# The down projection by a seven-product scheme on one NeuronCore

## The chip, the cores and the metric

The kernel runs on one core of one Trainium2 chip. The metric is device time in microseconds (us) of the whole program, the median of several runs. The engines are named as the profile names them: PE is TensorE (matmuls; PEld its weight loads), DVE VectorE, ACT ScalarE, POOL GpSimd, SP SyncE, which here issues the DMAs.

## The reference

One layer of a hybrid encoder on 1024 tokens of width 1024: gated attention and a state-space branch, cross-attention, then a squared-ReLU MLP with a hidden width of 4096, and a final norm. The change concerns the last matrix product alone:

```
h = rmsnorm(x, norm_ffn[i])
x = x + jnp.square(jax.nn.relu(h @ w_up[i])) @ w_down[i]
...
return rmsnorm(x, norm_final)
```

All is float32. The kernel multiplies float32 by three matmuls: an operand is split into a high half (a copy into the fp32r type) and a low half (the operand minus its high half), and high x high, high x low and low x high are added up in PSUM.

## The kernel before, in words

The up phase leaves u = relu(h w_up)^2, transposed, in DRAM as 32 rows of tiles `dr.u[m]`, 128 hidden channels by 1024 tokens. It multiplies by a seven-product scheme of Strassen's kind already (class `Up`), and parks 4 of the 8 token tiles of the residual x in DRAM (`dr.x1`).

The down phase (`down_phase`) multiplies u by w_down. It goes over the 4096 hidden channels in eight blocks of four tiles m. For a block it loads for each m a row of u and a row of w_down (512 KB each), splits them with `split_u` (ACT copies, DVE subtracts, two halves of 128x512) and `split_wd` (ACT copies, POOL subtracts, 128x1024), and then makes 16 output tiles of 128x512 (eight token tiles t, two column halves ch), with 4 x 3 matmuls each, in one of eight PSUM banks. DVE adds each bank to the residual in SBUF (`kx.x1[t]`, tiles x1 and xl). Block b + 1 is prepared while block b is multiplied. Even blocks lie in the four big tiles `kt` (each 128 x 4 x 2 x 512, 16 KB per partition), odd ones in tiles of their own (`u`, `wd`). The first block is split during the last three quads of the up phase. After the last block, each finished token tile is normed (`norm_stats`) and stored.

PE's instructions keep the order of the code. Those of the other engines and of the DMA queue are put in order by a scheduler when the program is built; each engine then runs its own list strictly from the top, and an instruction that waits holds up those behind it. A tile of a ring (`tag`, `bufs`) can be written again when the readers of its last use are done.

Of the kernel before, what the change touches and what calls it, by code (L numbers as in the profile page):

```python
# [16 lines left out]
P = 128  # L17
S = 1024
D = 1024
NT = 8  # L20
# [57 lines left out]
def mm3(kx, out, l, r, first, last):  # L78

    mm = kx.nc.tensor.matmul  # L80
    i = mm(out, l[0], r[0], start=first, stop=False)  # L81
# [4 lines left out]
    mm(out, l[1], r[0], start=False, stop=last)  # L86
# [7 lines left out]
def kt_pair(t, sl=slice(None)):  # L94
    return t[:, 0, sl], t[:, 1, sl]
# [224 lines left out]
class Group:  # L320
    def __init__(self, g):
        self.g, self.hs, self.cx = g, slice(4 * g, 4 * g + 4), []
# [604 lines left out]
def up_phase(kx, ins, dr, ok, grow, x1_low):  # L927

    nc, tc = kx.nc, kx.tc
    with tc.tile_pool(name="p4", bufs=1, reuse_waits="tile") as mp:  # L930
        a11, a12 = kx.h3

        def rows(c):
            xn = mp.tile([P, D], F32, tag="ld", bufs=2, name="xn")
            norm_rows(kx, mp, kx.x1[c], xn, grow)
            return xn

        def park(c):
            nc.sync.dma_start(dr.x1[c], kx.x1[c])

        xns = [rows(2), rows(3)]
        for c in range(4):
            xo_units(kx, ins, 1, ok, c, (0, 1))
            park(c)
            if c in (1, 2):
                norm_split(kx, xns[c - 1], [a11, a12], (c + 1) * P)
        x1_low.close()
        with tc.tile_pool(name="tp", bufs=1, side="right", reuse_waits="tile") as tp:
            up = Up(kx, ins, dr, mp, tp, {"a11": a11, "a12": a12}, grow)
            xns = [rows(4), rows(5)]  # L950
# [16 lines left out]
            stage, wd = [], []  # L967
            for n, b in enumerate(order):
                if n == 13:
                    us = down_us(kx)  # L970
                    raws = []

                    def load(src):
                        raws.append(mp.tile([P, D], F32, tag="ld", bufs=2, name="sraw"))
                        nc.sync.dma_start(raws[-1], src)

                    def u_part(j):
                        split_u(kx, None, us, j, raws.pop(0))

                    def w_part(j):  # L980
                        if j == 0:
                            wd.append(down_wd(kx))
                        split_wd(kx, None, wd[0][2 * j:2 * j + 2], j, raws.pop(0), nc.vector)
# [10 lines left out]
            wd.append(down_wd(kx))  # L994
            for j in range(2, 4):
                raw = mp.tile([P, D], F32, tag="ld", bufs=2, name="draw")
                split_wd(kx, ins, wd[1][2 * j - 4:2 * j - 2], j, raw, nc.vector if j == 2 else nc.gpsimd)
    return us, wd[0] + wd[1]


def down_us(kx):

    kts = [kx.mp.tile([P, 4, 2, 512], F32R, tag="kt", bufs=4, name="kt") for _ in range(2)]
    return [t[:, i] for t in kts for i in range(4)]


def down_wd(kx):

    t = kx.mp.tile([P, 4, 2, 512], F32R, tag="kt", bufs=4, name="kt").rearrange("p a b c -> p a (b c)")
    return [t[:, i] for i in range(4)]  # L1010


def split_u(kx, dr, us, m, raw):
    nc = kx.nc
    if dr is not None:
        nc.sync.dma_start(raw, dr.u[m])
    for h in range(2):
        t = us[2 * (m % 4) + h]
        rh = raw[:, h * 512:(h + 1) * 512]
        nc.scalar.activation(t[:, 0], rh, AF.Copy)  # L1020
        nc.vector.tensor_tensor(t[:, 1], rh, t[:, 0].bitcast(F32), ALU.subtract)


def split_wd(kx, ins, hl, m, raw, eng):
    nc = kx.nc
    if ins is not None:
        nc.sync.dma_start(raw, ins["wdn"][m])
    nc.scalar.activation(hl[0], raw, AF.Copy)
    eng.tensor_tensor(hl[1], raw, hl[0].bitcast(F32), ALU.subtract)
# [204 lines left out]
        self.kx.nc.sync.dma_start(self.x, self.dr.u[2 * b + 1][:, :512])  # L1234


def down_phase(kx, ins, dr, first, out):
    nc, tc = kx.nc, kx.tc
    V, A, G, PE = nc.vector, nc.scalar, nc.gpsimd, nc.tensor
    with tc.tile_pool(name="p6", bufs=1, reuse_waits="tile") as fp, \  # L1240
            tc.tile_pool(name="xl", bufs=1, side="right", reuse_waits="tile") as xp:
        NB = 8

        def block(b):
            if b % 2:
                us = [fp.tile([P, 2, 512], F32R, tag="u", bufs=8, name="u") for _ in range(8)]
                wd = [fp.tile([P, D], F32R, tag="wd", bufs=8, name="wd") for _ in range(8)]
            else:
                us, wd = down_us(kx), down_wd(kx) + down_wd(kx)
            for j in range(4):  # L1250
                m = 4 * b + j
                split_u(kx, dr, us, m, fp.tile([P, D], F32, tag="uraw", bufs=2, name="uraw"))
                split_wd(kx, ins, wd[2 * j:2 * j + 2], m, kx.wp.tile([P, D], F32, tag="raw", bufs=2, name="raw"), G)
            return us, wd
# [4 lines left out]
        nxt = first  # L1259
        gf = load_row(kx, kx.tabp, ins["gfin"], "tab", eng=nc.sync)  # L1260
        for b in range(NB):
            us, wd = nxt
            if b + 1 < NB:
                nxt = block(b + 1)
            for t in range(NT):
                for ch in range(2):
                    ps = kx.pp.tile([P, 512], F32, tag="p", name="dps")
                    cs = slice(ch * 512, (ch + 1) * 512)
                    for j in range(4):
                        mm3(kx, ps, kt_pair(us[2 * j + t // 4], slice((t % 4) * P, (t % 4) * P + P)),  # L1270
                            (wd[2 * j][:, cs], wd[2 * j + 1][:, cs]), j == 0, j == 3)
                    xh = kx.x1[t][:, cs]
                    V.tensor_tensor(xh, xh, ps, ALU.add)
                if b == NB - 1:
                    xn = kx.wp.tile([P, D], F32, tag="wop", bufs=6, name="xnf")
                    r = norm_stats(kx, fp, kx.x1[t], xn)
                    V.scalar_tensor_tensor(xn, kx.x1[t], r[:, 0:1], gf, ALU.mult, ALU.mult)
                    nc.sync.dma_start(out[0, t * P:(t + 1) * P], xn)


@with_exitstack
# [122 lines left out]
```

## Time and profile before

| what | value |
|---|---|
| median of 3 runs | 2484.73 us (2481.28 to 2490.82) |
| the profiled execution, its time | 2489.64 us |
| its span | 2487.9 us |
| first matmul of the down phase | 2131.82 us |
| last matmul of the down phase starts | 2479.77 us |

The span is the part of the execution that the profiler's records cover. Rows of groups read: line, engine, operation, output<-inputs, shapes and count, then busy time in us, the mean ns of one, and the engine's idle time before them with what ended it. Rows of the timeline read: start and duration in us, engine, line, operation, count, and in brackets idle time before. SPq is the DMA queue of SyncE.

### The profile page before, as it was taken

How to read it: one execution, taken by the hardware profiler on the slowest of the kernel's cores; microseconds unless marked ns; L12 is line 12 of the kernel's file. 1: busy time of each engine (PE TensorE's matmuls, PEld its weight loads, DVE VectorE, ACT ScalarE, POOL GpSimd, SP SyncE). 2: the span in 40 equal slices, each digit the busy share in tenths (PEclk: the TensorE clock that was granted, in tenths of full speed). 3: DMA queues.
4: the chain of work that ended last, by engine and by line, in shares of the span. 5: the costliest groups of instructions: out<-in, count | busy, mean ns of one | idle time of the engine just before them, and what ended most of it. 6: DMA issues, size and time to landing. Idle time of an engine off the chain costs nothing.

```text
span 2487.9 us, 32565 instructions
## 1 busy us (share of the span) xinstructions
PE 2400.1 (96%) x12156; PEld 1992.3 (80%) x12156; DVE 1349.9 (54%) x2048; ACT 1070.2 (43%) x2214; POOL 1049.3 (42%) x905
## 2 busy tenths in 40 slices
PE   7899999999999999999999999999989999999998
PEld 6688887878878788777777878888978887888887
DVE  5747566575765754565554242335675457454434
ACT  5436355463644544576674242225443333221211
POOL 4334536354453633444454444224585444231310
PEclk9999999999999999999999999999999999999999
DMA  6223223232322322111125363412343345432211
GB/s 226 77 65 123 68 85 102 69 119 60 111 80 82 112 65 71 50 46 50 52 71 209 131 216 126 180 43 77 119 148 123 106 148 186 154 135 85 100 53 68
DMA packets 154927, 260.47 MB, mean 105 GB/s; under 512 B 11793, under 2 KB 86673, under 8 KB 154769
## 3 DMA queue, kind: packets, MB, share of 16 engines
q1 hardware_dynamic: 83872, 219.58, 25.8%
q10 hardware_dynamic: 70896, 38.81, 5.5%
q8 instruction: 96, 1.57, 0.2%
q14 instruction: 63, 0.51, 0.1%
HBM read 210.90 MB, written 47.45 MB: 104 GB/s over the span
## 4 chain that ended last, share of the span: by engine, by line
PE 65%; DVE 11%; POOL 8%; ACT 7%; issue 5%; DMA 3%; SPq 0%; ACTq 0%; POOLq 0%; DVEq 0%
PE pb L1143 5%; PE dps L86 5%; PE dps L81 5%; PE dps L85 5%; PE mps L86 3%; PE mps L85 3%; PE mps L81 3%; PE pc L1143 3%; PE zp L85 2%; PE zp L81 2%; PE zp L86 2%; PE st L462 2%; POOL wlo L67 2%; DVE cx L350 2%; POOL prev L477 2%
## 5 line engine op out<-in xcount | busy, mean ns | idle before, releaser
L67 POOL TENSOR_TENSOR wlo<-raw,whi 128x1024 fp32r<-128x1024 f32 x142 | 349.9, 2465 | 595.9 <-ACT whi L66 561.0
L66 ACT ACTIVATE whi<-raw 128x1024 fp32r<-128x1024 f32 x144 | 152.0, 1056 | 256.3 <-PE mps L85 115.2
L81 PE MATMUL cps<-kt,whi 128*128 128x512 f32 x512 | 217.5, 425 | 8.6 <-DVE cx L350 8.6
L86 PE MATMUL cps<-kt,wlo 128*128 128x512 f32 x512 | 201.4, 393 | 0.0
L85 PE MATMUL cps<-kt,whi 128*128 128x512 f32 x512 | 200.9, 392 | 0.0
L81 PEld LDWEIGHTS cps<-kt,whi 128*128 128x128 f32 x512 | 97.4, 190 | 34.7 <-issue 16.0
L1089 POOL TENSOR_TENSOR wop<-w,wop 128x512 fp32r<-128x512 f32 x64 | 86.0, 1346 | 85.7 <-ACT wop L1088 75.8
L85 PEld LDWEIGHTS cps<-kt,whi 128*128 128x128 f32 x512 | 97.3, 190 | 26.3 <-issue 7.3
L86 PEld LDWEIGHTS cps<-kt,wlo 128*128 128x128 f32 x512 | 96.9, 189 | 20.9
L120 POOL TENSOR_TENSOR rr<-rv,mhalf 128x1 f32<-128x1 f32 (+1 forms) x50 | 38.6, 771 | 169.2 <-DVE rv L118 166.6
L81 PE MATMUL gps<-kt,whi 128*128 128x512 f32 x256 | 109.5, 428 | 0.0
L496 ACT ACTIVATE ef<-rows,ebias 128x128 f32<-128x128 f32 x256 | 83.2, 391 | 53.3 <-PE cb L511 49.8
L1143 PE MATMUL pb<-kt,wop 128*128 128x512 f32 x384 | 95.8, 399 | 9.6 <-ACT c L1197 9.2
L86 PE MATMUL mps<-yk,wlo 128*128 128x512 f32 x256 | 100.6, 393 | 4.1 <-POOL wlo L67 4.1
L680 POOL TENSOR_SCALAR t<-t,den 128x384 f32<-128x384 f32 (+1 forms) x128 | 69.1, 559 | 82.0 <-DVE den L678 65.7
L85 PE MATMUL mps<-yk,whi 128*128 128x512 f32 x256 | 100.5, 392 | 1.6 <-DVE yk L734 1.6
L86 PE MATMUL gps<-kt,wlo 128*128 128x512 f32 x256 | 101.8, 398 | 0.0
L85 PE MATMUL gps<-kt,whi 128*128 128x512 f32 x256 | 101.1, 395 | 0.0
L81 PE MATMUL mps<-yk,whi 128*128 128x512 f32 x256 | 100.5, 392 | 0.0
L86 PE MATMUL dps<-wd,u 128*128 128x512 f32 x256 | 99.7, 389 | 0.0
L86 PE MATMUL dps<-kt 128*128 128x512 f32 x256 | 99.7, 389 | 0.0
L85 PE MATMUL dps<-wd,u 128*128 128x512 f32 x256 | 99.7, 389 | 0.0
(373 smaller groups left out, 7124.8 us busy)
## 6 DMA issues: line engine op xcount, KB each, us to landing
rows<-d_cs ACTq DMA_DIRECT2D x128, 256.0 KB, 3.8
raw<-in_wssd_dram SPq DMA_DIRECT2D x48, 512.0 KB, 3.2
raw<-in_wup_dram SPq DMA_DIRECT2D x40, 512.0 KB, 3.6
raw<-in_wsb_dram SPq DMA_DIRECT2D x32, 512.0 KB, 3.2
d_u<-c SPq DMA_DIRECT2D x64, 256.0 KB, 2.1
raw<-in_wdn_dram SPq DMA_DIRECT2D x28, 512.0 KB, 4.2
uraw<-d_u SPq DMA_DIRECT2D x28, 512.0 KB, 4.1
x<-in_x_dram SPq DMA_DIRECT2D x16, 512.0 KB, 7.6
```

The costliest lines, as they stand in the source:

```text
L66: nc.scalar.activation(hi, raw, AF.Copy)
L67: (eng or nc.gpsimd).tensor_tensor(lo, raw, hi.bitcast(F32), ALU.subtract)
L81: i = mm(out, l[0], r[0], start=first, stop=False)
L85: mm(out, l[0], r[1], start=False, stop=False)
L86: mm(out, l[1], r[0], start=False, stop=last)
L350: V.scalar_tensor_tensor(acc[:, :S - o], ps[:, o:], cw(k), acc[:, :S - o], ALU.mult, ALU.add)
L462: PE.matmul(st[:, lo:hi], q.btok[:, c], xs.rearrange("p d h q -> p (d h q)")[:, lo:hi], start=True, stop=True)
L477: G.tensor_tensor(prev[:, c - 1, 1], prev[:, c - 1, 1], t, ALU.add)
L496: A.activation(ef[:, h], rows[:, 0, h], AF.Exp, bias=kx.ebias[:, b, j, 0, o:o + 1])
L680: G.tensor_scalar(t4[:, i, :n], t4[:, i, :n], den[:, i:i + 1], 1.0, ALU.mult, ALU.mult)
L1089: self.kx.nc.gpsimd.tensor_tensor(t[:, 1], src, t[:, 0].bitcast(F32), ALU.subtract)
L1143: self.kx.nc.tensor.matmul(ps, w[:, i, ks], act[:, k, j], start=start and k == 0 and m == 0, stop=k == 3 and m == 2, skip_group_check=True)
```

## The change

The down projection becomes: one plain block (tiles m = 0 to 3), three groups of eight tiles (16 to 23, 24 to 31, 4 to 11), one plain block (12 to 15). A group holds u and w_down as 2 x 2 blocks: a11, a12, a21, a22 (token half, four tiles of the group) and b11, b12, b21, b22 (four tiles, column half). Instead of eight block products it makes seven, of the operands below, in the order 1, 2, 6, 5, 7, 3, 4:

- 1: a11 b11; 2: a12 b21; 6: s2 t6; 5: s1 t5; 7: x y; 3: s4 b22; 4: a22 t4
- s1 = a21 + a22, s2 = s1 - a11, s4 = a12 - s2, x = a11 - a21
- t5 = b12 - b11, t6 = b22 - t5, t4 = b21 - t6, y = b22 - b12

Products 1, 6, 7 and 4 add up in four banks (pb), 2 alone and then 5 and 3 in four others (pc); after each product DVE adds the bank as it stands to the output quarter that is due: 1 and 2 to the first, 6 and 3 to the second, 5 and 7 to the fourth, 4 to the third. A product is 4 row tiles x 4 x 3 = 48 matmuls. Its split operands fill two kt tiles; there are four, so two products' worth. Sums are made in place in the loaded rows (`row`), x and y in tiles of their own (`xy`). `early(j)` makes x, y, s1 and t5 of tile j (DVE and POOL), `s2`, `t6`, `s4`, `t4` are dealt to DVE and POOL by the parity of j. In each split ACT copies and DVE subtracts the left operand, and POOL subtracts the right one.

```diff
+class Pair:
+    ORDER = (1, 2, 6, 5, 7, 3, 4)
...
+    def row(self, tag, src):
+        if tag == "wop":
+            t = self.kx.wp.tile([P, D], F32, tag="wop", bufs=6, name="row")
+        else:
+            t = self.fp.tile([P, D], F32, tag=tag, bufs={"k1": 10, "k2": 6}[tag], name="row")
+        self.kx.nc.sync.dma_start(t, src)
+        return t
+
+    def load(self, j):
+        m = self.ms[j]
+        self.u[j] = self.row("k1" if j < 4 else "k2", self.dr.u[m])
+        self.w[j] = self.row("k1" if j < 4 else "wop", self.ins["wdn"][m])
...
+    def early(self, j):
+        V, G, op = self.kx.nc.vector, self.kx.nc.gpsimd, self.op
+        pool = self.fp if j < 2 else self.kx.wp
+        self.xy[j] = pool.tile([P, D], F32, tag="raw", bufs=2, name="xy")
+        return [lambda: op(V, "x", "a11", "a21", ALU.subtract, j), lambda: op(G, "y", "b22", "b12", ALU.subtract, j),
+                lambda: op(V, "a21", "a21", "a22", ALU.add, j), lambda: op(G, "b12", "b12", "b11", ALU.subtract, j)]
+
+    def eng(self, j, odd):
+        return self.kx.nc.gpsimd if j % 2 != odd else self.kx.nc.vector
+
+    def s2(self, j):
+        self.op(self.eng(j, 0), "a11", "a21", "a11", ALU.subtract, j)
...
+    def split(self, n):
...
+        self.lr = lt, rt = kt_tile(self.kx), kt_tile(self.kx)
+
+        def step(t, name, eng, j):
+            src = self.half(name, j)
+            nc.scalar.activation(t[:, j, 0], src, AF.Copy)
+            eng.tensor_tensor(t[:, j, 1], src, t[:, j, 0].bitcast(F32), ALU.subtract)
+
+        return [lambda t=t, name=name, eng=eng, j=j: step(t, name, eng, j) for j in range(4)
+                for t, name, eng in ((lt, left, nc.vector), (rt, right, nc.gpsimd))]
...
 def down_phase(kx, ins, dr, first, out):
...
+        pairs = [Pair(kx, ins, dr, fp, range(16 + 8 * b, 24 + 8 * b)) for b in range(2)]
+        pairs.append(Pair(kx, ins, dr, fp, range(4, 12)))
...
+        tiles = [(t, ch, bank()) for t in range(4, 8) for ch in range(2)]
+        units = [u for j in range(4) for u in p.early(j)]
+        split1 = p.split(1)
+        units += split1
+        for j in range(4):
+            for i, (t, ch, ps) in enumerate(tiles):
+                part(ps, us, wd, t, ch, j, j == 0, j == 3)
+                if j == 3:
+                    add(t, ch, ps)
+            if j < 2:
+                deal(units, j, 2)
...
+        for b, p in enumerate(pairs):
...
+            for i, n in enumerate(Pair.ORDER):
+                lt, rt = p.lr
+                if i < 6:
+                    units = p.split(Pair.ORDER[i + 1])
+                elif nxt:
+                    units = nxt.split(1)
...
+                if i == 3:
+                    for j in range(4):
+                        units.insert(3 * j + 2, lambda j=j: (p.t4(j), nxt.load(j + 1) if nxt and j < 3 else None))
+                if i == 4:
+                    if nxt:
+                        units += nxt.early(0)
...
+                if i == 6 and nxt:
+                    units += nxt.early(2) + nxt.early(3)
+                ps = pb if n in (1, 6, 7, 4) else pc
+                t0, ch = {1: (0, 0), 2: (0, 0), 6: (0, 1), 5: (4, 1), 7: (4, 1), 3: (0, 1), 4: (4, 0)}[n]
+                for t in range(4):
+                    deal(units, t, 4)
+                    ts = slice(t * P, (t + 1) * P)
+                    for k in range(4):
+                        for m, (x, y) in enumerate(((0, 0), (0, 1), (1, 0))):
+                            PE.matmul(ps[t], lt[:, k, x, ts], rt[:, k, y], start=n in (1, 2, 5) and k == 0 and m == 0,
+                                      stop=k == 3 and m == 2, skip_group_check=True)
+                    add(t0 + t, ch, ps[t])
```

The second half of the first plain block goes over its four tiles j outermost, so that its first w tile is free before its end. The kt tiles of that block are taken in another order (`down_tiles`). In the last group the rows of the last block are loaded and split in between (`fload`, `fsplit_w`).

The scheduler sets where the splits and sums stand. Three places show it. In the first, POOL in the down phase before: nothing but the subtractions of w rows, a whole row each.

```order
L1029 TENSOR_TENSOR wd_18781<-raw_18818,wd_18780 128x1024
L1029 TENSOR_TENSOR kt_19048<-raw_19056,kt_19048 128x1024
L1029 TENSOR_TENSOR kt_19048<-raw_19066,kt_19048 128x1024
L1029 TENSOR_TENSOR kt_19049<-raw_19076,kt_19049 128x1024
L1029 TENSOR_TENSOR kt_19049<-raw_19086,kt_19049 128x1024
```

POOL after, while the second group's product 5 runs: kt_19869 is the right operand of product 7, the rows with xy_19956 to row_19877 are y and t5 of the next group's first two tiles.

```order
L1306 TENSOR_TENSOR kt_19869<-xy_19390,kt_19869 128x512
L1271 TENSOR_TENSOR xy_19956<-row_19642,row_19638 128x512
L1306 TENSOR_TENSOR kt_19869<-xy_19465,kt_19869 128x512
L1271 TENSOR_TENSOR row_19638<-row_19638 128x512
L1271 TENSOR_TENSOR xy_20031<-row_19646,row_19877 128x512
L1306 TENSOR_TENSOR kt_19869<-xy_19548,kt_19869 128x512
L1271 TENSOR_TENSOR row_19877<-row_19877 128x512
L1306 TENSOR_TENSOR kt_19869<-xy_19549,kt_19869 128x512
```

Eight POOL instructions stand up to the last subtraction that product 7 needs, four of them for the next group.

POOL after, at the second change of group: four subtractions for product 4 (not shown), y and t5 of the next group's last two tiles (the first row here is the last of these), then the right operand of the next group's product 1 (kt_20113) and sums between, a whole row of w for the last plain block (wd), and the right operand of product 2 (kt_20201).

```order
L1271 TENSOR_TENSOR row_19921<-row_19921 128x512
L1306 TENSOR_TENSOR kt_20113<-row_19638,kt_20113 128x512
L1271 TENSOR_TENSOR row_19638<-row_19642,row_19638 128x512
L1306 TENSOR_TENSOR kt_20113<-row_19877,kt_20113 128x512
L1271 TENSOR_TENSOR row_19875<-row_19875 128x512
L1306 TENSOR_TENSOR kt_20113<-row_19899,kt_20113 128x512
L1271 TENSOR_TENSOR row_19899<-row_20055,row_19899 128x512
L1306 TENSOR_TENSOR kt_20113<-row_19921,kt_20113 128x512
L1271 TENSOR_TENSOR row_19919<-row_19919 128x512
L1032 TENSOR_TENSOR wd_20562<-row_20202,wd_20561 128x1024
L1306 TENSOR_TENSOR kt_20201<-row_19642,kt_20201 128x512
L1271 TENSOR_TENSOR row_19642<-row_19642,row_19638 128x512
```

The sums for later products have moved between the subtractions of products 1 and 2, where the code has them in later stages. The first change of group reads alike, without the wd row.

DVE before, at the change from one block to the next: additions out of PSUM (dps) with a few subtractions of u.

```order
L1273 TENSOR_TENSOR x1_14315<-x1_14315,dps_19018 128x512
L1021 TENSOR_TENSOR kt_19046<-uraw_19050,kt_19046 128x512 x2
L1273 TENSOR_TENSOR x1_14315<-x1_14315,dps_19032 128x512
L1021 TENSOR_TENSOR kt_19046<-uraw_19060,kt_19046 128x512 x2
L1273 TENSOR_TENSOR xl_18756<-xl_18756,dps_19090 128x512
```

DVE after, while the first group's product 4 runs: kt_19546 is the left operand of the second group's product 1, the rows of L1271 are its s2 and t6, and x1 with dps are the additions of product 4.

```order
L1306 TENSOR_TENSOR kt_19546<-row_19070,kt_19546 128x512
L1271 TENSOR_TENSOR row_19070<-row_19070 128x512
L1306 TENSOR_TENSOR kt_19546<-row_19309,kt_19546 128x512
L1331 TENSOR_TENSOR x1_14309<-x1_14309,dps_19060 128x512
L1306 TENSOR_TENSOR kt_19546<-row_19331,kt_19546 128x512
L1306 TENSOR_TENSOR kt_19546<-row_19353,kt_19546 128x512
L1271 TENSOR_TENSOR row_19331<-row_19331 128x512
L1271 TENSOR_TENSOR row_19311<-row_19080,row_19311 128x512
L1331 TENSOR_TENSOR x1_14311<-x1_14311,dps_19061 128x512
L1271 TENSOR_TENSOR row_19355<-row_19514,row_19355 128x512
L1331 TENSOR_TENSOR x1_14313<-x1_14313,dps_19062 128x512
L1331 TENSOR_TENSOR x1_14315<-x1_14315,dps_19063 128x512
```

The last two additions now stand behind row_19355, a sum that overwrites b11 of the fourth tile and so waits for POOL's last subtraction of product 1.

More of the change, by code (lines that the diff above doesn't have):

```diff
@@ L966, in up_phase @@
             up.start(order, 5)
-            stage, wd = [], []
+            stage = []
             for n, b in enumerate(order):
                 if n == 13:
-                    us = down_us(kx)
+                    us, wd = down_tiles(kx)
+                    wd = wd_views(wd[0])
                     raws = []
@@ L1241, in down_phase @@
             tc.tile_pool(name="xl", bufs=1, side="right", reuse_waits="tile") as xp:
[L1242 to L1254, printed above, removed]
         for t in range(4):
@@ L1258, in down_phase, with bank @@
             nc.sync.dma_start(kx.x1[t], dr.x1[t])
-        nxt = first
-        gf = load_row(kx, kx.tabp, ins["gfin"], "tab", eng=nc.sync)
[L1261 to L1268, printed above, removed]
-                    for j in range(4):
[L1270 to L1278, printed above, removed]
+        def bank():
+            return kx.pp.tile([P, 512], F32, tag="p", name="dps")
@@ new lines, in part, with add, deal @@
+        def part(ps, us, wd, t, ch, j, first, last):
+            cs = slice(ch * 512, (ch + 1) * 512)
+            mm3(kx, ps, kt_pair(us[2 * j + t // 4], slice((t % 4) * P, (t % 4) * P + P)),
+                (wd[2 * j][:, cs], wd[2 * j + 1][:, cs]), first, last)
+        def add(t, ch, ps):
+            xh = kx.x1[t][:, ch * 512:(ch + 1) * 512]
+            V.tensor_tensor(xh, xh, ps, ALU.add)
+        def deal(units, i, n):
+            for unit in units[len(units) * i // n:len(units) * (i + 1) // n]:
+                unit()
@@ new lines, in down_phase @@
+        pairs = [Pair(kx, ins, dr, fp, range(16 + 8 * b, 24 + 8 * b)) for b in range(2)]
+        pairs.append(Pair(kx, ins, dr, fp, range(4, 12)))
+        p = pairs[0]
+        for j in range(4):
+            p.load(j)
+            p.load(4 + j)
+        us, wd = first
+        for t in range(4):
+            for ch in range(2):
+                ps = bank()
+                for j in range(4):
+                    part(ps, us, wd, t, ch, j, j == 0, j == 3)
+                add(t, ch, ps)
+        tiles = [(t, ch, bank()) for t in range(4, 8) for ch in range(2)]
@@ L1281, in hybrid_encoder @@
+        for t in range(NT):
+            for ch in range(2):
+                ps = bank()
+                for j in range(4):
+                    part(ps, fu, fw, t, ch, j, j == 0, j == 3)
+                add(t, ch, ps)
+            xn = kx.wp.tile([P, D], F32, tag="wop", bufs=6, name="xnf")
+            r = norm_stats(kx, fp, kx.x1[t], xn)
+            V.scalar_tensor_tensor(xn, kx.x1[t], r[:, 0:1], gf, ALU.mult, ALU.mult)
+            nc.sync.dma_start(out[0, t * P:(t + 1) * P], xn)
 @with_exitstack
```

86 lines of the change are left out of this document (75 added, 11 removed).

## The prediction, made before the changed kernel was run

> **What bounds the kernel now.** I read the page first, then the groups of instructions between 2132 and 2482 us, then the first and last matmul of the stage in the timeline.
>
> ```profile
> span 2487.9 us, 32565 instructions
> PE 2400.1 (96%) x12156; PEld 1992.3 (80%) x12156; DVE 1349.9 (54%) x2048; ACT 1070.2 (43%) x2214; POOL 1049.3 (42%) x905
> ...
> L86 PE MATMUL dps<-wd,u 128*128 128x512 f32 x256 | 99.7, 389 | 0.0
> L86 PE MATMUL dps<-kt 128*128 128x512 f32 x256 | 99.7, 389 | 0.0
> L1273 DVE TENSOR_TENSOR x<-x,dps 128x512 f32<-128x512 f32 x64 | 44.0, 687 | 101.0 <-PE dps L86 101.0
> L1021 DVE TENSOR_TENSOR kt<-uraw,kt 128x512 fp32r<-128x512 f32 x24 | 31.9, 1368 | 6.3 <-ACT kt L1020 6.1
> L1029 POOL TENSOR_TENSOR kt<-raw,kt 128x1024 fp32r<-128x1024 f32 x12 | 30.7, 2570 | 100.0 <-ACT kt L1028 100.0
> L1020 ACT ACTIVATE kt<-uraw 128x512 fp32r<-128x512 f32 x24 | 13.8, 622 | 101.6 <-PE dps L86 88.9 <-DMA uraw<-d_u 12.7
> ```
> ```profile
> 2131.82 0.39 PE L81 MATMUL dps<-kt 128*128 128x512 f32 x1
> ...
> 2173.77 0.39 PE L86 MATMUL dps<-kt 128*128 128x512 f32 x1
> ...
> 2479.77 0.39 PE L86 MATMUL dps<-wd,u 128*128 128x512 f32 x1
> ```
>
> TensorE is the bound: in this stage its groups have 0.0 idle ahead of them, VectorE waits 101 us for it in one group alone, and ScalarE and GpSimd wait about as long. There are 6 groups of 256, 1536 matmuls; from the first start to the last, (2479.77 - 2131.82) / 1535 = 0.2267 us each. Every matmul taken away here is 0.2267 us of the end, as long as the engines that feed TensorE keep up. Whether they do is the whole question.
>
> **The matmuls.** The built program has 1392 matmuls into these banks: 192 + 3 x 336 + 192. That is 144 fewer: **-32.6 us**. Stationary and moving operands both still lie in kt tiles, and the groups from kt and from wd,u have the same 389 ns, so I keep 0.2267. One product is 48 matmuls, 10.88 us; one of its four row tiles is 2.72 us.
>
> **The feeding.** Before, each of 28 pairs of rows (u and w) cost GpSimd (POOL) one 128x1024 subtraction and VectorE (DVE) two of 128x512. Now each product needs four 128x512 subtractions on each of the two, and each group of eight tiles 32 sums and differences besides, half on each: 28 + 16 = 44 instructions on each per group. These rows show what one costs, alone and beside the other engine.
>
> ```profile
> 2081.14 1.30 POOL L1089 TENSOR_TENSOR wop<-w,wop 128x512 fp32r<-128x512 f32 x1 [3.29 <-ACT wop L1088]
> 2082.39 1.75 POOL L1089 TENSOR_TENSOR wop<-raw,wop 128x512 fp32r<-128x512 f32 x1
> ...
> 2081.62 1.37 DVE L1021 TENSOR_TENSOR kt<-sraw,kt 128x512 fp32r<-128x512 f32 x1 [0.36 <-ACT kt L1020]
> 2082.91 1.78 DVE L1117 TENSOR_TENSOR w<-raw,w 128x512 f32<-128x512 f32 x1
> ...
> 2108.38 4.23 POOL L1089 TENSOR_TENSOR wop<-w,wop 128x512 fp32r<-128x512 f32 x3 [3.40 <-ACT wop L1088]
> 2111.39 0.68 DVE L1187 TENSOR_TENSOR c<-x,pc 128x512 f32<-128x512 f32 x1
> ...
> 2176.38 5.22 POOL L1029 TENSOR_TENSOR kt<-raw,kt 128x1024 fp32r<-128x1024 f32 x2 [21.39 <-ACT kt L1028]
> ```
>
> They alternate. The first POOL instruction runs 2081.14 to 2082.44; the VectorE one issued at 2081.62 does not end until 2082.99. POOL's second starts 1.25 us after its first and takes 1.75 us, that is 0.45 us longer; VectorE's next again ends only 0.55 us behind it (2084.69 against 2084.14). So of a VectorE instruction with two SBUF operands and a POOL instruction, one waits for the other. An addition out of PSUM (2111.39, inside POOL's three) keeps its 0.68. I count **1.25 us for a POOL instruction and 0.45 us more for each two-SBUF VectorE instruction ready beside it**; the 128x1024 pair (5.22 = 2.36 + 2.86) gives the same 0.45. For a whole group that is 44 x 1.70 = 74.8 us beside 7 x 10.88 = 76.2 us of TensorE: it just fits on average. But only four kt tiles exist, so work can't be done ahead, and it is not spread evenly.
>
> When may a split begin, and when must it end? The tiles of product n+1 are those of n-1, free as n begins.
>
> ```profile
> 2174.19 1.15 ACT L1020 ACTIVATE kt<-uraw 128x512 fp32r<-128x512 f32 x2 [21.68 <-PE dps L86]
> 2175.25 1.05 ACT L1028 ACTIVATE kt<-raw 128x1024 fp32r<-128x1024 f32 x1
> ```
>
> The matmul of 2173.77 ends at 2174.16 and ScalarE starts at 2174.19. The last matmul of a product ends 0.16 after the next has begun; then 0.03 to ScalarE, 0.53 for the left copy (two take 1.15, the second 0.62), 0.62 for the right, 0.08 to POOL (2176.30 to 2176.38): POOL's first subtraction starts 1.42 us into a product. TensorE needs the last one (the low half of the fourth right piece) at matmul 10 of the first row tile: 10 x 0.2267 = 2.27 us into the next product, 13.15 us after the start of this one. So with n POOL instructions up to that one and m VectorE ones beside them, the stall is 1.42 + 1.25 n + 0.45 m - 13.15, where positive. From the order:
>
> - Four subtractions alone (n = 4, m = 4): 8.2. Hidden, and lateness is made up. These are three or four of the seven.
> - First product of a group, with the sums for products 3 and 4 among the subtractions (n = 7, m = 6): 12.9. Just hidden in the first group.
> - Product 5, where the four early POOL differences for the next group stand among the subtractions for 7 (n = 8, m = 7): 14.57, **1.42 us** late, twice.
> - From product 3 through 4 to the next group's product 1: four subtractions, four early differences, then subtractions and sums mixed: n = 15 and m = 12 from the start of product 3: 25.57, against 10.88 + 13.15 = 24.03. **1.54 us**, twice.
> - There the second heavy stage follows without a pause: n = 8, m = 7 more, 13.15 us, so 38.72 against 24.03 + 1.54 + 10.88 = 36.45: **2.27 us**, twice.
> - Before the last group a whole 128x1024 subtraction (wd) stands in that row too: 2.36 + 0.45 = **2.81 us**, once. The other three wd subtractions follow stages of four and are made up before product 7 (1.42 + 6.8 + 7.1 = 15.3, 4.4 late; then 4.4 + 6.8 = 11.2 of 13.15).
>
> Together 2 x (1.42 + 1.54 + 2.27) + 2.81 = **13.3 us**.
>
> **The clock.** Ahead of the last group's product 2 the wait is 2.27 + 2.81 = 5.08 us, but its pieces come 3.40 us apart (two POOL and two VectorE instructions) and TensorE uses each up in 0.68: two gaps of some 2.4 and 2.7 us. What such a gap does:
>
> ```profile
> 924.40 1.12 PE L511 MATMUL cb<-xtok,ef 128*128 128x64 f32 x8 [2.28 <-DVE ef L499]
> ...
> 921.80:925.30 3.50, 1.22 (x11) 1.05 (x10) 2.84 (x4) 1.61 (x6) 3.42 (x7) 1.00 0.00 0
> 925.30:928.70 3.40, 3.40 (x8) 2.08 (x8) 3.16 (x6) 2.12 (x9) 1.55 (x3) 0.50 0.46 129
> ...
> 2083.00:2086.50 3.50, 2.21 (x10) 1.50 (x10) 3.47 (x4) 0.00 (x0) 1.14 (x1) 1.00 0.69 200
> 2086.50:2090.00 3.50, 3.50 (x17) 2.84 (x16) 2.80 (x4) 2.37 (x5) 1.29 (x1) 1.00 0.46 179
> ```
>
> In rows of windows the last three numbers are granted clock, DMA share and GB/s. A gap of 2.28 us, in 3.5 us with TensorE busy for 1.22, is followed by 3.4 us at half clock; 3.5 us with 2.21 busy are not. I add one such stretch, 3.4 / 2 = **1.7 us**, for that place and none for the single shorter gaps. [...]
>
> **What is hidden.** ScalarE has 8 copies per product, 8 x 0.53 = 4.3 of 10.88 us. VectorE has 116 additions out of PSUM instead of 128. Those of row tiles 2 and 3 of product 4 stand behind a sum that waits for POOL's last subtraction (25.57); they end near 27.4, and TensorE wants the banks at 28.7: hidden with 1.3 us to spare. SyncE issues as many loads as before; the 18 that follow the up phase are 9.4 MB:
>
> ```profile
> GB/s 69 187 249 96 206 333 401 53 377 266 63 299 235 137 0 0 87 157 380 214 363 421 410 321 180 176 8 0 0 0 0 5 168 182 182 236 397 221 12 145
> uraw<-d_u SPq DMA_DIRECT2D x12, 512.0 KB, 4.2
> ...
> xl<-d_x SPq DMA_DIRECT2D x4, 512.0 KB, 6.4
> ```
>
> At some 400 GB/s, as in slices 22 and 23 of 3 us, they take 24 us from 2135, and the first split waits anyway until the first w tile is free (96 + 48 matmuls, 2164.5). Inside a group, four loads wait for buffers that product 4's split frees; the first is issued 3.4 us into product 3 and, at 4.2, lands at 7.6, when POOL reaches it at about 8. That cover is 0.4 us; at 6.4 us to landing it would add up to 1.8 us, twice. The end (last plain block, norm, store) is unchanged.
>
> **Sum.** -32.6 + 13.3 + 1.7 = **-17.6 us**. The profiled execution took 2489.64 us around its span of 2487.9, 4.9 above the median of 2484.73; from the median, **2467.1 us** (-0.7%).
>
> **Rivals.** A measurement here tells about 0.5% (12.4 us) from no change.
>
> *Feeding is hidden* (22%). If VectorE instructions fall into pauses of POOL, m is 0 and the worst stages need 1.42 + 10 = 11.4 of 13.15 and 20.2 of 24.03; nothing stalls. For it: averages fit. Against it: rows at 2082 and 2176 show every pair colliding. It gives 2484.7 - 32.6 = 2452.1.
>
> *The waiting engine waits for the whole instruction* (20%): 0.69 instead of 0.45, as VectorE's 687 and 0.68 rows last. Then the stalls are 1.2 (first group), 2 x 3.1, 2 x 4.4, 2 x 4.0 and 3.05, 27.2 us, and 1.7 us of clock: 2481. For it: nothing but the length of the rows; against it: 1.75 - 1.30. [...]
>
> *Slower* (8%). VectorE and GpSimd become the bound of every product if a pair costs over 2.07 us: 44 x 2.07 = 91.1, 15 above 76.2 in each of three groups, and 45 us are the 32.6 gained and 12.4 more.
>
> ```profile
> L1089 POOL TENSOR_TENSOR wop<-raw,wop 128x512 fp32r<-128x512 f32 x9 | 14.7, 1631 | 12.6 <-ACT wop L1088 12.5
> ```
>
> Halves of rows, as here, have a mean of 1.63 us on POOL between 2000 and 2132 us; with 0.69 that is 2.32, 102.1 per group, 3 x 25.9 - 32.6 = 45 us, 2530. Against it: those 1.63 hold waits that I count already.
>
> **Chances.** My forecast, 2460 to 2472, has 50%; the two ends, 2452.1 and 2481, hold 42% and the range reaches both. Faster by over 0.5% means below 2472.3: 50 + 22 = 72%. Same: 20%. Slower: 8%.
>
> **What would show it.** Right: 1392 matmuls at 0.227 us; TensorE's idle 13 to 15 us in all, put down to POOL, ahead of products 7, 1 and 2 and nowhere else, longest before the last group's product 2, where the clock falls to 0.5 for 3.4 us; POOL instructions of 1.25 and 1.70 us by turns. Wrong: idle before every product (the slower rival), none (the first), waits for a load (the cover of 0.4 us), or matmuls spaced over 0.23 us.

## The result, and the profile after

The changed kernel takes 2469.5 us, the median of four runs (2469.22 to 2473.64), against 2484.85 (2481.28 to 2490.82) of the kernel before in the same comparison: a ratio of 0.994, 95% interval 0.9918 to 0.9962. The forecast was 2467.1. The profiled execution, the slowest of the four, took 2473.64 us around a span of 2471.9, 16.0 below the span before.

The page's first lines, the first and the last matmul of the down phase in the timeline, and its costliest groups between 2130 and 2465 us:

```profile
span 2471.9 us, 32466 instructions
PE 2371.6 (96%) x12012; PEld 1965.7 (80%) x12012; DVE 1456.7 (59%) x2120; ACT 1107.9 (45%) x2310; POOL 1199.7 (49%) x1013
```
```profile
2130.18 0.39 PE L81 MATMUL dps<-kt 128*128 128x512 f32 x1
...
2463.76 0.39 PE L86 MATMUL dps<-wd,kt 128*128 128x512 f32 x1
```
```profile
L1427 PE MATMUL dps<-kt 128*128 128x512 f32 x1008 | 234.1, 394 | 12.8 <-POOL kt L1306 12.7
L1306 POOL TENSOR_TENSOR kt<-row,kt 128x512 fp32r<-128x512 f32 x72 | 117.5, 1653 | 22.8 <-ACT kt L1305 22.8
L1306 DVE TENSOR_TENSOR kt<-row,kt 128x512 fp32r<-128x512 f32 x72 | 93.6, 1327 | 1.6 <-ACT kt L1305 1.6
L1271 POOL TENSOR_TENSOR row<-row 128x512 f32<-128x512 f32 x36 | 56.1, 1559 | 6.4 <-issue 2.5 <-DVE kt L1306 2.5
L1271 DVE TENSOR_TENSOR row<-row 128x512 f32<-128x512 f32 x36 | 54.6, 1528 | 16.5 <-POOL kt L1306 10.6 <-DMA row<-d_u 5.8
L86 PE MATMUL dps<-kt 128*128 128x512 f32 x64 | 24.9, 389 | 0.0
```

The 1008 matmuls of the seven-product groups now have idle time ahead of them, 12.8 us, and nearly all of it ends with POOL's right subtractions (`kt` of line 1306). The plain blocks still have 0.0. POOL's subtractions and sums last 1653 and 1559 ns on average, neither 1.25 nor 1.70: some stand alone, most beside a VectorE instruction (of the 84 right subtractions 17 last 1.3 to 1.4 us, the other 67 some 1.7 to 1.8).

From first to last matmul the phase takes 2463.76 - 2130.18 = 333.6 us, before 347.95. Of the 32.6 that 144 matmuls are worth 18.2 came back as time beyond a spacing of 0.2267; another 1.6 us were won before the phase began. I cut the phase at the first matmul of each product; one that waits for nothing takes 10.88 us. Rows of windows of the profiled run: length, busy time of PE, PEld, DVE, ACT and POOL, granted clock, DMA share, GB/s.

```profile
2206.83:2217.71 10.88, 10.88 (x49) 9.01 (x48) 10.33 (x9) 4.28 (x8) 9.37 (x6) 1.00 0.46 186
2217.71:2230.26 12.55, 11.19 (x49) 8.94 (x48) 12.55 (x14) 4.28 (x8) 10.65 (x7) 1.00 0.00 0
2252.02:2264.96 12.94, 11.18 (x49) 8.94 (x48) 11.10 (x11) 4.28 (x8) 12.15 (x9) 1.00 0.01 1
2264.96:2280.01 15.05, 12.80 (x49) 10.11 (x48) 15.01 (x15) 4.27 (x8) 12.58 (x8) 0.89 0.00 1
...
2336.09:2348.85 12.76, 11.17 (x49) 8.94 (x48) 10.91 (x10) 4.28 (x8) 12.60 (x8) 1.00 0.13 41
2348.85:2366.03 17.18, 12.77 (x49) 9.83 (x48) 16.46 (x15) 4.28 (x8) 14.59 (x10) 0.90 0.00 1
```

The first row is a product that waits for nothing. The second is product 7 of the first group, then come products 1 and 2 of the second group, then 1 and 2 of the last. Product 7 of the second group takes 12.55 as well, product 2 of the first 11.25, product 1 of the first 10.98, and every other product 10.88. Each wait of over 1 us stands ahead of matmul 10 of a product's first row tile, the one that needs POOL's last subtraction; only the last group's product 2 waits at matmul 7 as well. The clock falls in the product 2 of both later groups (0.89, 0.90).

The place at 2267 to 2272 us in the timeline:

```profile
2266.30 1.61 POOL L1271 TENSOR_TENSOR row<-row 128x512 f32<-128x512 f32 x1
2266.70 3.44 DVE L1271 TENSOR_TENSOR row<-row 128x512 f32<-128x512 f32 x2
2267.88 1.71 POOL L1306 TENSOR_TENSOR kt<-row,kt 128x512 fp32r<-128x512 f32 x1
2269.55 1.73 POOL L1271 TENSOR_TENSOR row<-row 128x512 f32<-128x512 f32 x1
...
2269.64 2.59 PE L1427 MATMUL dps<-kt 128*128 128x512 f32 x6 [2.25 <-POOL kt L1306]
```

A sum for a later product (2266.30) stands ahead of the subtraction that TensorE waits for (2267.88 to 2269.59), and two VectorE sums run beside them; the two POOL instructions last 1.61 and 1.71 us where one alone lasts about 1.3. TensorE goes on 0.05 us after the subtraction.

### The profile page after: what moved, and what is told of

It is laid out like the page before. It is cut to its first block, busy times and chain, and to the rows that moved or that the text cites. A ratio compares the mean times of both kernels' runs of the same rounds, so it can differ in the third digit from the quotient of the medians.

```text
span 2471.9 us, 32466 instructions
## 1 busy us (share of the span) xinstructions
PE 2371.6 (96%) x12012; PEld 1965.7 (80%) x12012; DVE 1456.7 (59%) x2120; ACT 1107.9 (45%) x2310; POOL 1199.7 (49%) x1013
## 4 chain that ended last, share of the span: by engine, by line
PE 57%; DVE 13%; POOL 11%; ACT 8%; issue 6%; DMA 4%; ACTq 0%; POOLq 0%; SPq 0%; DVEq 0%
PE pb L1146 6%; PE dps L1427 5%; PE mps L86 3%; PE mps L85 3%; PE mps L81 3%; PE pc L1146 3%; PE zp L85 2%; PE zp L81 2%; PE zp L86 2%; POOL wlo L67 2%; PE st L462 2%; DVE cx L350 2%; POOL prev L477 2%; POOL kt L1306 1%; ACT whi L66 1%
## 5 line engine op out<-in xcount | busy, mean ns | idle before, releaser
L1427 PE MATMUL dps<-kt 128*128 128x512 f32 x1008 | 234.1, 394 | 12.8 <-POOL kt L1306 12.7
L1427 PEld LDWEIGHTS dps<-kt 128*128 128x128 f32 x1008 | 190.8, 190 | 56.0 <-POOL kt L1306 16.2
L1305 ACT ACTIVATE kt<-row 128x512 fp32r<-128x512 f32 x144 | 77.2, 618 | 156.7 <-PE dps L1427 119.7
L1306 POOL TENSOR_TENSOR kt<-row,kt 128x512 fp32r<-128x512 f32 x72 | 117.5, 1653 | 22.8 <-ACT kt L1305 22.8
L85 PE MATMUL mps<-yk,whi 128*128 128x512 f32 x256 | 100.7, 393 | 0.2 <-DVE yk L734 0.2
```

The costliest lines, as they stand in the source:

```text
L1305: nc.scalar.activation(t[:, j, 0], src, AF.Copy)
L1306: eng.tensor_tensor(t[:, j, 1], src, t[:, j, 0].bitcast(F32), ALU.subtract)
L1427: PE.matmul(ps[t], lt[:, k, x, ts], rt[:, k, y], start=n in (1, 2, 5) and k == 0 and m == 0, stop=k == 3 and m == 2, skip_group_check=True)
```

## The experiments

The phase from its first to its last matmul tells these kernels apart better than the median does, because what comes ahead of it wanders by some us (first matmul at 2125.50 to 2135.03 in the table; last section). Median and interval of the ratio are those of each kernel's own comparison; the kernel before had 2487.43 us beside e1 to e4, 2491.0 beside e5 and e8 and 2486.78 beside e10, so medians of different rows are compared by their ratios.

| kernel | first matmul | phase | span | median (n) | ratio to before |
|---|---|---|---|---|---|
| before | 2131.82 | 347.95 | 2487.9 | 2484.85 (4) | |
| after | 2130.18 | 333.59 | 2471.9 | 2469.5 (4) | 0.994 (0.9918 to 0.9962) |
| e1, POOL in the code's order | 2125.50 | 318.98 | 2452.6 | 2456.78 | 0.988 (0.9861 to 0.9898) |
| e2, DVE too | 2130.56 | 319.29 | 2457.9 | 2458.89 | 0.9882 (0.9865 to 0.99) |
| e3, no DVE sums | 2132.97 | 323.54 | 2464.6 | 2466.9 (2) | 0.9916 (0.9895 to 0.9937) |
| e4, no POOL sums | 2128.28 | 315.31 | 2451.7 | 2453.53 (2) | 0.9862 (0.9841 to 0.9883) |
| e5, no wd row | 2132.11 | 331.60 | 2471.8 | 2473.2 (2) | 0.9933 (0.9912 to 0.9954) |
| e8, right operand first | 2135.03 | 322.12 | 2465.2 | 2464.94 (4) | 0.9889 (0.9867 to 0.9912) |
| e10, one s2 later | 2127.01 | 318.33 | 2453.4 | 2458.94 (4) | 0.989 (0.9873 to 0.9907) |

**e1: POOL in the order of the code.** My theory: the waits come from where the scheduler put sums and early differences, ahead of subtractions that are due. The rival: POOL has too much work whatever its order.

```diff
-            down_phase(kx, ins, dr, up_phase(kx, ins, dr, ok, grow, x1_low), out)
+            first = up_phase(kx, ins, dr, ok, grow, x1_low)
+        with tc.manual_schedule(engines={mybir.EngineType.PE, mybir.EngineType.Pool}):
+            down_phase(kx, ins, dr, first, out)
```

> Same work as the changed kernel; in the down phase POOL's instructions keep the order of the code, so sums stand after the subtractions of products 3, 4 and 1, and two at most between those of the others. Lock theory (a POOL instruction 1.25 us, 0.45 us more for each two-SBUF VectorE instruction beside it, deadline 13.15 us): at most n = 6 and m = 6 stand up to the last subtraction of a product, 1.42 + 7.5 + 2.7 = 11.6; after product 1 of the next group, with four early differences behind it, 4 us late + 5 x 1.25 + 5 x 0.45 = 12.5. No stall; TensorE's idle in the stage goes from 18 us to under 2, 2451 to 2454 us. Rival (the amount of POOL's and VectorE's work stalls TensorE, not its order): 2469.5 us, as the changed kernel.

The phase fell by 14.6 us with the same instructions, and POOL is busy for as long (1196.3 us for 1199.7). It is the order. TensorE's waits between 2100 and 2464 us in e1 (engine line waited for: us in total, times, longest):

```profile
PEld dps L1427 <- DVE kt L1306: 4.2, 6, 1.2
...
PE dps L1427 <- DVE kt L1306: 1.7, 3, 0.7
...
PEld dps L1427 <- POOL kt L1306: 0.2, 1, 0.2
```

The same of the changed kernel:

```profile
PEld dps L1427 <- POOL kt L1306: 16.2, 8, 2.8
...
PE dps L1427 <- POOL kt L1306: 12.7, 7, 2.4
```

POOL is gone from TensorE's waits but for 0.2 us. The 3.64 us that e1 has left, all at products 2 and 6 of the later groups, are waits for VectorE but for those 0.2. The expectation had no stall and under 2 us; that part missed. By its ratio this kernel beats both the kernel before and the changed one: 0.988 (up to 0.9898) against 0.994 (from 0.9918).

**e2: VectorE in the order of the code as well** (`mybir.EngineType.DVE` added to e1's set).

> As the run with POOL in the order of the code, and VectorE's instructions in the order of the code too: its splits and sums stand between the additions of a product, the last subtraction behind the third addition, some 9.5 us into the product and ended by 11.3, where 13.4 is the deadline. Lock theory: no stall, 2451 to 2454 us. Rival (VectorE behind the additions comes late): over 1 us idle before each product, 20 x 1 us, 2470 us or more.

A phase of 319.29: the 4.0 us lost moved to product 6 of the two later groups, and TensorE's waits from VectorE to POOL. The theory had expected no stall and the rival over 1 us ahead of each product; neither came out, and nothing was gained over e1.

**e3: VectorE's sums left out.** This leaves out the 16 sums of a group on VectorE, so that product 7 reads a21 where x should be; POOL keeps its list.

```diff
     def op(self, eng, out, x, y, alu, j):
+        if eng is self.kx.nc.vector:
+            return
...
-        return [lambda: op(V, "x", ...), lambda: op(G, "y", ...), lambda: op(V, "a21", ...), lambda: op(G, "b12", ...)]
+        return [lambda: op(G, "y", ...), lambda: op(G, "b12", ...)]
...
-7: ("x", "y")
+7: ("a21", "y")
```

> Leaves out the 16 sums and differences per group that VectorE makes (product 7 takes a21 as its left operand); POOL keeps all 44 instructions in the order of the changed kernel. Lock theory: m falls to 3 in product 5 (1.42 + 10 + 1.35 = 12.8, no stall), to 6 from product 3 on (22.9 of 24.0), then 34.7 of 34.9; only the wd subtraction before the last group's product 2 is left, 2.6 us and perhaps 1.7 of clock. Idle 3 to 4.5 us instead of 18, 2454 to 2457 us, and POOL's instructions mostly 1.25 to 1.3 us. Rival (POOL's own work is too long for its place, whatever VectorE does): the same 18 us, 2469.5 us.

2466.9 lies outside what my theory expected, and near the rival. The phase puts it elsewhere: the time beyond pace is 8.2 us instead of 18.2, where the theory had 3 to 4.5 and the rival 18. Product 7 and product 1 wait no longer, as expected; since POOL's own list is the same, it was VectorE's sums beside it that made it late there. Only product 2 of the two later groups still loses time, 1.45 and 6.74 us. The last group's, a row of windows of e3:

```profile
2341.19:2358.80 17.61, 14.09 (x49) 10.77 (x48) 8.39 (x8) 4.28 (x8) 13.19 (x10) 0.81 0.00 1
```

The expectation had counted six VectorE instructions fewer up to product 1 and came out just in time at product 2 (34.7 of 34.9). With four fewer, a count made after the run, the same formula comes nearer, though it still falls short: up to product 1 nothing waits (25.57 - 1.8 = 23.77 of 24.03); then eight POOL instructions with four subtractions beside them, 11.8, end at 35.57 of 34.91, 0.66 late, and 3.47 with the wd row. The gaps were 1.31 and 1.74 + 2.11 = 3.85, and a half-clock stretch of 6.8 us costs most of the rest. The phase fell by 10.05 us and the span by 7.3, since the phase began 2.8 us later than in the changed kernel; the medians, of different comparisons, differ by 2.6 us. POOL's own load as the cause is refuted by e1.

**e4: POOL's sums left out.** The same for POOL's 16 sums; product 7 reads b12 where y should be.

```diff
     def op(self, eng, out, x, y, alu, j):
+        if eng is self.kx.nc.gpsimd:
+            return
...
```

> Leaves out POOL's 16 sums and differences per group (product 7 takes b12 as its right operand); VectorE keeps its 44. Both the lock theory and the theory of POOL's load: n = 4 everywhere, 8.2 us of 13.15, no stall, 2451 us, the gain of the matmuls alone. Rival (VectorE's sums are what comes late): the stalls stay, 2465 us or more.

Not one product waits: 315.31 us, 32.64 below the phase before, exactly 144 times 0.2267. This is what the change could bring at most with 144 matmuls fewer.

**e5: the wd row left out.** In the last group one of the four wd subtractions is replaced by a second copy on ScalarE.

```diff
-                    split_wd(kx, None, hl, j, fraw[j], G)
+                    if j == 0:
+                        nc.scalar.activation(hl[0], fraw[j], AF.Copy)
+                        nc.scalar.activation(hl[1], fraw[j], AF.Copy)
+                    else:
+                        split_wd(kx, None, hl, j, fraw[j], G)
```

> Leaves out the one wd subtraction (128x1024) that stands on POOL between the last group's products 1 and 2 (its output gets a second ScalarE copy instead); nothing else moves on POOL. First to last matmul of the down phase took 333.59 us in the changed kernel, 33.6 of these (315.3 + 18.2). If that row costs what I charged (2.81 us), the last group's product 2 falls from 17.19 us to between 14.4 and 15.1, the 15.05 of the second group's product 2, and the phase to 331. Rival: what makes the last group's product 2 longer than the second group's is the clock and not the row; then it stays at 16 to 17 us. A second question: whether the half-clock stretch stays after one gap of about 2.4 us as in the second group (yes by my reading).

The last group's product 2 in e5:

```profile
2350.95:2365.96 15.01, 12.78 (x49) 10.08 (x48) 14.99 (x15) 4.27 (x8) 12.57 (x8) 0.89 0.00 1
```

15.01 for 17.18, and the same as the second group's 15.05: the row costs 2.17 us there, not 2.81. The clock still falls in both, so the wd row was not what made it fall. The ratio, 0.9933 for 0.994, is too coarse for these 2 us.

**e6, e7, e9: what a gap does to the clock.** In e4, where nothing waits, the last right subtraction of every second product is repeated, so that TensorE gets gaps of chosen length. POOL is in the code's order. The lines that repeat it:

```diff
...
+            more = (5.32 + gap) * (gap > 0 and j == 3 and eng is nc.gpsimd)
+            while more > 0.25:
+                w = 512 if more > 1.3 else min(512, 16 * int(32 * (more - 0.14) / 1.11))
+                eng.tensor_tensor(t[:, j, 1, :w], src[:, :w], t[:, j, 0, :w].bitcast(F32), ALU.subtract)
+                more = more - 1.25 if more > 1.3 else 0
             eng.tensor_tensor(t[:, j, 1], src, t[:, j, 0].bitcast(F32), ALU.subtract)
...
```

> Leaves out POOL's sums as e4 did (there no product waited, 10.88 us each), and repeats the last right subtraction of every second product so often that TensorE should wait 1.2, 1.6, 1.9, 2.1, 2.3, 2.5, 2.8, 3.2 and 3.6 us, in this order, ahead of products 6, 7 and 4 of the three groups (third, fifth and seventh). If the length of the gap decides and the bound lies near 2.3 us, as my row of 2.28 us says, five of the nine are followed by 3.4 us at half clock (1.7 us each): phase 315.3 + 21.2 + 8.5 = 345.0 us. [...] If not length alone but how much of a 3.41 us window is idle decides, gaps of 1.9 to 3.2 us drop the clock or not by where they fall.

> As e6, with gaps of 2.5, 1.9, 3.0, 2.2, 2.7, 1.4, 2.4, 3.4 and 2.0 us in this order, so that like lengths fall elsewhere in time. Bound near 2.3 us by length: five stretches (2.5, 3.0, 2.7, 2.4, 3.4), phase 315.3 + 21.5 + 8.5 = 345.3 us. [...] By windows: among gaps of 2.2 to 2.7 us some drop the clock and some do not, and those that do are the ones that lie inside one window of the clock's record.

The gaps came out 1.3 to 2.8 us longer than meant, 2.77 to 5.56, since repeats of one tile wait 0.08 us for each other and meet VectorE's instructions; phases 372.2 and 372.6. Every gap of 3.58 us or more was followed by a fall of the clock. The one of 2.77 (e6) was not, which speaks against a bound near 2.3 us, while behind the changed kernel's single gap of 2.41 us the clock fell: no one bound on the length fits both. In the clock record of the changed kernel's whole execution the half-clock stretches last 3.413, 6.827 or 10.24 us, but for the last, which ends with the record, and all begin on one grid of 3.413 us (those of the down phase, at 2270.06 and 2355.40 us, are 25 steps apart). So I laid this grid over the down phases of every changed kernel so far, and took TensorE's idle time of each window from the starts of its matmuls. In windows at full clock up to 1.92 us idle nothing followed; from 2.04 on each of 22 was followed by a window at half clock. e9 tests this on nine new gaps.

> As e6 (POOL's sums left out, the last right subtraction of every second product repeated), with the repeats set by what e6 and e7 showed so that all nine gaps come out near 2.6 us (2.4 to 2.9). Theory from the runs so far: the clock goes by windows of 3.413 us on a fixed grid; a window in which TensorE is idle for more than 2.0 us (1.92 had no consequence, 2.04 had) is followed by one at half clock, whatever the length of the gap. Then a gap of 2.6 us drops the clock unless a border cuts it so that neither part passes 2.0: about 5 of 9, 3 to 7, and in every case the idle of the window tells which. Rival by length, bound near 2.3 us: all nine. [...] Phase 315.3 + 23.4 + 1.7 for each stretch: 347 by windows, 354 or 339 by the rivals.

The nine came out at 2.09 to 2.70 us. Two were followed by a half-clock stretch, those of 2.35 and 2.70; seven were not, one of 2.41 among them. That is fewer than the 3 to 7 that I counted, but in all nine the window tells it: idle of 2.15 and 2.20 where the clock fell, 1.80 and less where it did not. The phase is 340.43: 315.31, 20.6 of gaps, some 0.13 more behind each, and two stretches; the expectation's 354 and 339 stand for nine and for none. Windows on the grid, first of e9 and then of the changed kernel; the second number is PE's busy time (each matmul counted with its 0.39, so 0.1 to 0.2 more than by the starts), the third from the end the clock:

```profile
2192.10:2195.51 3.41, 1.77 (x8) 1.13 (x6) 2.73 (x3) 3.41 (x8) 3.25 (x3) 1.00 0.22 68
2195.51:2198.92 3.41, 2.80 (x12) 2.35 (x13) 2.03 (x2) 0.41 (x1) 3.41 (x4) 1.00 0.69 239
2277.43:2280.84 3.41, 1.32 (x6) 1.08 (x7) 1.45 (x2) 1.95 (x4) 3.33 (x4) 1.00 0.80 226
2280.85:2284.26 3.41, 3.41 (x10) 2.63 (x9) 3.33 (x3) 0.00 (x0) 3.41 (x3) 0.50 0.43 118
```
```profile
2266.65:2270.06 3.41, 1.16 (x6) 0.66 (x5) 3.41 (x3) 2.79 (x6) 3.41 (x3) 1.00 0.01 2
2270.06:2273.48 3.42, 3.42 (x10) 2.68 (x9) 3.42 (x6) 0.00 (x0) 3.42 (x3) 0.50 0.00 0
2253.00:2256.41 3.41, 1.65 (x8) 1.07 (x7) 1.61 (x3) 3.41 (x7) 3.33 (x4) 1.00 0.00 0
2256.41:2259.83 3.42, 3.42 (x16) 2.80 (x16) 3.39 (x5) 0.09 (x1) 3.34 (x3) 1.00 0.00 0
```

In e9 a border cuts the gap of 2.41 us: PE is busy for 1.77 and 2.80 us on its two sides, and the clock stays at 1.00. The gap of 2.35 leaves one window with 1.32, and the next is at 0.50. In the changed kernel the gap of 2.41 us lies whole in one window, with PE busy for 1.16, and the next is at 0.50; that of 1.92 ahead of product 1 leaves 1.65 busy, and the clock stays at 1.00. The theory by length falls.

**e8 and e10: the rest of e1.** Both keep POOL in the order of the code, as e1. In e8 each split takes the right operand's copy first; in e10 the fourth s2, a POOL instruction, moves from product 1 to product 2.

```diff
e8
-                for t, name, eng in ((lt, left, nc.vector), (rt, right, nc.gpsimd))]
+                for t, name, eng in ((rt, right, nc.gpsimd), (lt, left, nc.vector))]
e10
-                    for j in range(4):
+                    for j in range(3):
                         units.insert(3 * j + 2, lambda j=j: p.s2(j))
...
                     units = [u for j in range(4) for u in (lambda j=j: p.t6(j), units[2 * j], units[2 * j + 1])]
+                    units.insert(9, lambda: p.s2(3))
```

> e1 (POOL in the order of the code; phase 318.98 us, 3.6 of them waits, all ahead of products 2 and 6 at the two changes of group) with one more edit: in each split the right operand's copy comes before the left one's, so that POOL starts 0.53 us earlier. If the offset of a split's start is a term of the wait, as I counted it, product 2 waits 0.5 us less in both groups and the phase falls to 317.9. Rival: POOL is late there anyway and takes up no earlier start; 319.0. Time about that of e1, 2454 to 2458.

> e1 with the fourth s2 (on POOL) moved from product 1 to product 2, just ahead of the subtraction that reads it. e1's waits left are 1.2 to 1.4 us ahead of product 2 and 0.4 ahead of product 6, at each of two changes of group (3.64 us of a phase of 318.98). If POOL's place in the row is what counts, product 2 waits 1.25 to 1.7 us less, that is not at all, and product 6 still waits about 0.4 (one row more, two of lateness less): phase 316 to 317. Rival: DVE is late there as much as POOL; 319. Time 2453 to 2457, not to be told from e1's by the median.

Both miss. In e8 product 2 of the second group waits 0.35 us less (1.43 to 1.08), but that of the last 0.77 more, and a new gap of 2.51 us stands ahead of the last group's product 1: the scheduler, still free on VectorE, put sums ahead of left subtractions there. In e10 product 2 still waits 1.45 and 1.19 us, against 1.43 and 1.55 in e1; product 6 waits 0.2 for 0.35. TensorE's waits in e8, then in e10:

```profile
PE dps L1427 <- DVE kt L1306: 4.5, 4, 2.3
...
PEld dps L1427 <- DVE kt L1306: 7.6, 8, 2.8
```
```profile
PE dps L1428 <- DVE kt L1306: 1.5, 2, 0.7
...
PEld dps L1428 <- DVE kt L1306: 3.8, 6, 1.2
```

In e10 the rival was right. In e8 neither side was: the phase is 322.12, and TensorE's waits end with VectorE, not with POOL. With POOL in order it is VectorE that is late at a change of group, and neither of these two edits takes that away. e8's gap of 2.51 us is cut by a border into windows with 1.44 and 1.19 us idle, and the clock does not fall.

## Why the prediction came out right

**The matmuls** (-32.6): right. e4 shows it alone, 32.64.

**The feeding** (+13.3): right in mechanism and place, a little small. Without the clock the products took 18.25 - 3.3 = 14.9 us beyond 10.88 each. Step by step, forecast and time lost: first group's product 2 0 and 0.37; product 7 1.42 and 1.67, twice; product 1 1.54 and 2.06, then 1.88; product 2 of the second group 2.27 and 2.41; product 2 of the last 5.08 and 4.7 (gaps of 2.19 and 2.55). For the last two the time lost is the gaps alone; what stands behind them is counted with the clock. What the terms lacked is mostly the step from POOL's last instruction to TensorE in pace: 0.05 us until the matmul starts, and about 0.15 more behind it (product 7: a gap of 1.52, a loss of 1.67). The wd row was the one term too large: 2.17 for 2.81 (e5).

**0.45 us for each pair**: bore out. POOL's starts in the timeline above are 1.58 and 1.67 us apart with VectorE beside, 0.33 and 0.42 above 1.25; five in a row from 2187.11 us on are 1.70 to 1.79 apart. With 0.69, the rival, product 7 would have waited 3.1 us; it lost 1.67. VectorE itself pays more: the two sums beside them last 3.44 us, where one while POOL waits for a load lasts 0.69 (at 2136.35 us).

**The clock** (+1.7): the wrong step. It was forecast for one place, and fell in two, for 1.8 and 1.6 us. I read a row with a gap of 2.28 us as a bound on length, and took the single wait of 2.27 ahead of the second group's product 2 to be below what counts. What told the falls apart in the down phases of these runs is how much of one window at full clock of the 3.413 us grid was idle: 2.04 us or more where the clock fell, 1.92 or less where it did not. The forecast could not know where the borders would fall: an estimate from 2.04 and 3.413 us is that a gap of 2.41 us with a border at random leaves 2.04 or more in one window in about half of the cases, so the number of places in one profiled execution is partly chance.

**Hidden work**: bore out for TensorE's own waits: no matmul of the down phase waits for a DMA, for a copy or for a bank. VectorE's sums wait 5.8 us for loads (group row above), most of it in the first plain block, where TensorE has no idle time. At the two changes of group VectorE waits 0.67 and 0.37 us for a row and POOL 0.08 and 0.22, so the forecast's cover of 0.4 us was just used up. Whether a part of product 1's 2.06 and 1.88 us comes from there was not told apart.

**The sum.** -32.6 + 14.9 + 3.3 - 1.6 = -16.0 us between the two profiled spans, forecast -17.6. The last term, the earlier start of the phase, was in no step and comes from the stages ahead, where TensorE's instructions are the same: feeding and clock together were forecast 3.2 us too small, and half of that was made good by it. The changed stage alone gained 14.4 us and not 17.6; that the number came as near as it did is in part luck. By the medians the difference is 15.35 us, and 2469.5 lies 2.4 above the forecast. The hidden rival (2452.1) is what e4 reaches by leaving work out. What I did not ask is whether the waits are a property of the change or of its order: e1 wins the gain but for 3.6 us by the order alone.

## What to carry to other kernels

A feeding engine that fits on average must be counted stage by stage: the instructions that stand ahead of the last one a stage needs, each with the price that a neighbour engine adds (here 0.33 to 0.54 us on POOL's 1.25 beside VectorE), against that stage's deadline. If a scheduler put work for later stages among them, set the order of that engine by hand before giving up the change, and look at the other feeding engine next: here it became the late one (in e1 all of TensorE's waits but 0.2 us are for VectorE). Compare kernels by the stage that was changed, from its first to its last matmul, when what lies ahead of it wanders by more than the change is worth.

## What the runs showed of the hardware that I had not expected

In the clock records of the kernel before and of the changed one every half-clock stretch begins on a grid of 3.413 us and lasts one, two or three steps of it, but for the last, which ends with the record. In the down phases of the changed kernels 24 of 24 windows at full clock with 2.04 us or more of TensorE's time idle were followed by one at half clock, and none of over 50 with 0.4 to 1.92. A gap of 2.77 us was free (e6), and one of 2.35 cost some 1.7 us (e9). In a window that was itself at half clock less was enough: the seven with 0.77 us idle or more (matmuls counted 0.427 us apart) were followed by a second one, as in e3 and in six windows of e6 and e7, and those with 0.76 or less were not, the changed kernel's last product 2 among them at 0.76. With other matmuls, in the earlier stages, PE's busy time alone does not tell: in the kernel before, the window from 525.92 us on, with PE busy for 1.73 us, was followed by one at half clock, and that from 631.74 on, with 1.71, was not.

A stage that the change does not touch moved the whole by 4 to 5 us. TensorE's wait for a weight near 1455 us, in the kernel before, in the changed one and in e1:

```profile
PE mps L86 <- POOL wlo L67: 4.1, 1, 4.1
```
```profile
PE mps L86 <- POOL wlo L67: 4.8, 1, 4.8
```
```profile
PE mps L86 <- POOL wlo L67: 0.5, 1, 0.5
```

Behind the two long ones the clock falls, for 3.4 us in the kernel before and for 6.8 in the changed one; in e1 and e4 neither happened, and they reach the down phase 2 to 6 us earlier than before and after. e8, whose program is e1's up to the down phase, has the long wait (4.8 us). Why it comes and goes was not looked into.
